# A Strassen FFN: stored block outputs added to x1 in DRAM, and the raw-weight rings at the change from plain tiles to blocks

## The chip, the cores and the metric

The kernel runs on 1 core of one Trainium2 chip. The metric is the device time of one execution in microseconds. Three runs of the kernel before took 898.76, 900.21 and 903.96 us; the median is 900.21.

## The reference

The layer is a hybrid of pooling mixer and mLSTM, followed by a SwiGLU FFN. All of the change is in the FFN's half, so the rest is named and left out:

```python
D_MODEL, SEQ = 1024, 512
D_FF = -(-8 * D_MODEL // (3 * 256)) * 256      # 2816 = 22 tiles of 128

def _swiglu(h, w_in, w_out):
    g, u = jnp.split(h @ w_in, 2, axis=-1)
    return (jax.nn.silu(g) * u) @ w_out
...
x1 = x + gate1 * (mixer(...) @ w_out_proj)
h  = _modulate(_rmsnorm(x1, ...), shift2, scale2)
x  = x1 + gate2 * _swiglu(h, w_ffn_in, w_ffn_out)
out = final rmsnorm(x)
```

## The kernel before

Every fp32 product is made from two rounded parts, high and low: three matmuls, wh·ah, wh·al and wl·ah (`mm3`). ScalarE casts the high part, VectorE subtracts it to get the low one (L158/L159, L177/L178, `split`); for some parts ScalarE writes the negated high part and an accumulating DMA of GpSimd's queue (POOL) adds the raw weight from DRAM (L1035/L1036, `direct` with a name in `sent`).

The FFN's 22 tiles of d_ff go in these steps. Tiles 0 to 2 are made with plain matmuls. Every later pair (one d_ff tile, gate and up rows together) is a `Pair`: seven products in the manner of Strassen instead of eight, four in `front` (A11, S1, S2, A12) and three in `back` (S3, S4, A22), of 12 matmuls of 128x256 each. `prepare` loads its two raw weights (`wr`, a ring of 3, and `ur`, a ring of 2) and makes seven high/low parts. Tile 3 is the pair `third`. Then a plain product brings tiles 0 to 3 through w_ffn_out into x1: for each of its 8 row blocks j a chunk of 512 columns is loaded into `wr` (into `ur` for j = 0), and the updated x1[j] is stored to DRAM as x1d[j] (L1443/L1446). Behind it x1's buffers close and those of the blocks open.

Two blocks follow, of the d_ff tiles from c0 = 4 and c0 = 10 on: three times an `Even` and an `Odd` pair (called E4, O5, and so on here), whose results are seven operand sets in `bo`, and then four `Out` pairs, which are the Strassen product with w_ffn_out over these six tiles. Their rows are scaled and stored to DRAM as od[c0] (L1236, L1240). The low part of A11 comes by accumulating DMA too for an `Odd` behind the block's first (L1179). Then come six plain pairs, P16 to P21, and a last plain product with the weights wl_0 to wl_7 over their tiles, with the final norm. For that, x1 is loaded back from x1d (L1472, two row blocks after each of P17 to P20), and 16 accumulating DMAs add od[4] and od[10] into it in SBUF (L1477), all issued behind P21's A22.

What sets the order: each engine runs its instructions in program order. `run` writes out the pairs so that a pair's front goes between the back products of the pair ahead, and prepares one pair ahead. Outside the part under `manual_schedule` a scheduler places the instructions on the engines; `issue_after` holds a group back until a named instruction. SP issues the plain loads and POOL the accumulating ones and the stores, each in its own order, and an instruction that waits there (for a buffer to come free) holds all behind it.

Names and lines: L188 to L190 are the matmuls of `mm3`; L1049 and L1050 VectorE's sums for S1 and S2 from `ur` and `wr`, L1056/L1057 those for S3/S4; L1124 VectorE's sum after S3, L1129 the one after S4, L1133 the one after A22, which ends a plain pair's value before its split into `act`; L1415 the update of x1.

## Time and profile before

| what | value |
|---|---|
| median of 3 runs | 900.21 us (898.76 to 903.96) |
| the profiled execution's own time | 899.67 us |
| its span | 897.9 us |
| PE busy | 874.6 us |
| mean granted clock of PE | 0.993 |
| DMA traffic | 134.59 MB, mean 150 GB/s |

The profile's times are of one execution and count from the span's start. A row of a timeline has start, duration, engine, line, operation, output<-input, and in brackets the idle time of the engine just before it with what ended it. PE is TensorE's matmuls, PEld its weight loads, DVE is VectorE, ACT ScalarE, POOL GpSimd. SPq is the queue of DMA issues on SyncE; its times are issues, not landings. A row of DMA issues has the transfer, the count, the size and the microseconds from issue to landing.

In the profile the plain product runs from about 573 to 603 us, the first block to about 690, the second to about 780, the pairs P16 to P21 to about 850.

### The profile page before, as it was taken

Reading aid. Unit: us, or ns where it says so; the run is one execution under the profiler, and the core shown is the slowest. Engines: PE = TensorE matmul, PEld = TensorE weight load, DVE = VectorE, ACT = ScalarE, POOL = GpSimd, SP = SyncE. Lnnn points to the kernel's source line nnn. Section 1 sums busy time; section 2 is a strip of 40 time slices with the busy share of each in tenths; the row PEclk is TensorE's granted clock in tenths of the full one; section 3 lists DMA queues with packets and bytes.
Section 4 is the critical chain, followed back from the end, with each engine's and each line's share of the span. In section 5 each row is a group of like instructions: output and inputs, shape, how many; then the busy total and the mean of one; then the engine's idle time right before and its main releaser. Section 6 shows DMA issues by size and latency. Waiting matters only on the chain.

```text
span 897.9 us, 15849 instructions
## 1 busy us (share of the span) xinstructions
PE 874.6 (97%) x6112; PEld 805.4 (90%) x6112; DVE 652.8 (73%) x1292; ACT 470.7 (52%) x919; POOL 98.1 (11%) x137
## 2 busy tenths in 40 slices
PE   9999999999999999999999999999999999998896
PEld 8689798899889998889988899879999999998896
DVE  4678677768876788667886659578888788856544
ACT  4454453545445453354545456446757775755442
POOL 0000000110000100001000000031202220221510
PEclk9999999999999999999999999999999999998999
DMA  9863021445352642526354710379637863794862
GB/s 350 317 201 99 25 71 60 164 129 153 106 177 66 194 112 76 191 69 199 98 153 154 276 48 25 94 211 239 142 103 218 218 147 99 223 283 103 181 127 95
DMA packets 48557, 134.59 MB, mean 150 GB/s; under 512 B 5440, under 2 KB 9824, under 8 KB 47456
## 3 DMA queue, kind: packets, MB, share of 16 engines
q1 hardware_dynamic: 38208, 112.06, 39.0%
q0 software_dynamic: 10272, 21.50, 11.7%
q8 instruction: 48, 0.79, 0.3%
q14 instruction: 29, 0.24, 0.1%
HBM read 123.56 MB, written 9.98 MB: 149 GB/s over the span
## 4 chain that ended last, share of the span: by engine, by line
PE 85%; DVE 6%; DMA 3%; ACT 3%; issue 2%; DVEq 0%; SPq 0%; ACTq 0%
PE ps L188 10%; PE ps L189 10%; PE ps L190 10%; PE ps L198 8%; PE ps L195 8%; PE ps L196 8%; PE pat L348 3%; PE ps L579 3%; PE ps L580 3%; PE ps L581 3%; PE pat L189 2%; PE pat L188 2%; PE pat L190 2%; PE pat L793 2%; PE pat L795 2%
## 5 line engine op out<-in xcount | busy, mean ns | idle before, releaser
L195 PE MATMUL ps<-a,wh 128*128 128x512 f32 x272 | 106.5, 392 | 0.0
L196 PE MATMUL ps<-a,wh 128*128 128x512 f32 x272 | 106.3, 391 | 0.0
L158 ACT CAST wh<-wr 128x1024 fp32r<-128x1024 f32 (+3 forms) x69 | 66.7, 969 | 63.4 <-PE ps L196 34.8
L159 DVE TENSOR_TENSOR wl<-wr,wh 128x1024 fp32r<-128x1024 f32 (+3 forms) x69 | 78.2, 1133 | 28.7 <-ACT wh L158 17.5
L198 PE MATMUL ps<-a,wl 128*128 128x512 f32 x272 | 68.0, 391 | 0.0
L196 PEld LDWEIGHTS ps<-a,wh 128*128 128x128 f32 x272 | 51.1, 188 | 10.2
L198 PEld LDWEIGHTS ps<-a,wl 128*128 128x128 f32 x272 | 50.9, 188 | 10.4
L195 PEld LDWEIGHTS ps<-a,wh 128*128 128x128 f32 x272 | 51.1, 188 | 10.1
L188 PE MATMUL ps<-hp,oh 128*128 128x256 f32 x176 | 50.8, 289 | 8.7 <-DVE tmp L1124 8.1
L1036 POOL DMA_DIRECT2D ol<-in_wffi x42 | 37.1, 882 | 146.6 <-ACT ol L1035 61.5
L188 PE MATMUL ps<-hp,gh 128*128 128x256 f32 x176 | 49.8, 283 | 2.9 <-ACT pat L1086 2.9
L190 PE MATMUL ps<-hp,ol 128*128 128x256 f32 x176 | 50.3, 286 | 0.0
L189 PE MATMUL ps<-hp,oh 128*128 128x256 f32 x176 | 50.2, 285 | 0.0
L189 PE MATMUL ps<-hp,gh 128*128 128x256 f32 x176 | 49.0, 278 | 0.0
L190 PE MATMUL ps<-hp,gl 128*128 128x256 f32 x176 | 48.9, 278 | 0.0
L177 ACT CAST gh<-sg 128x1024 fp32r<-128x1024 f32 (+1 forms) x27 | 26.7, 989 | 41.5 <-DVE sg L1050 26.5
L538 DVE SCALAR_TENSOR_TENSOR pb<-pb,crow_s 128x1024 f32<-128x1024 f32 x32 | 39.1, 1239 | 11.9 <-DMA pb<-in_wada_b 11.8
L188 PEld LDWEIGHTS ps<-hp,oh 128*128 128x128 f32 x176 | 34.6, 197 | 9.4 <-DVE tmp L1124 8.5
L793 PE MATMUL pat<-vh,Sp 128*128 128x258 f32 x144 | 41.1, 285 | 0.0
L794 PE MATMUL pat<-vl,Sp 128*128 128x258 f32 x144 | 40.7, 283 | 0.0
L795 PE MATMUL pat<-vh,Sp 128*128 128x258 f32 x144 | 40.7, 282 | 0.0
L178 DVE TENSOR_TENSOR gl<-sg,gh 128x1024 fp32r<-128x1024 f32 (+1 forms) x27 | 30.9, 1145 | 11.6 <-ACT gh L177 11.6
(422 smaller groups left out, 3031.2 us busy)
## 6 DMA issues: line engine op xcount, KB each, us to landing
wr<-in_w SPq DMA_DIRECT2D x42, 512.0 KB, 3.6
pb<-in_wada_b SPq DMA_DIRECT2D x32, 512.0 KB, 4.3
wr<-in_wffi SPq DMA_DIRECT2D x25, 512.0 KB, 4.8
ol<-in_wffi POOLq DMA_DIRECT2D x42, 256.0 KB, 5.8
ur<-in_wffi SPq DMA_DIRECT2D x19, 512.0 KB, 4.2
ada<-in_wada_a SPq DMA_DIRECT2D x8, 1024.0 KB, 9.9
wr<-in_wffo SPq DMA_DIRECT2D x16, 384.0 KB, 5.2
wr<-in_wout SPq DMA_DIRECT2D x8, 512.0 KB, 3.7
```

The source lines that it names most:

```text
L158: nc.scalar.copy(wh, raw[:, :n])
L159: V.tensor_sub(wl, raw[:, :n], wh.bitcast(F32))
L188: nc.tensor.matmul(dst, wh, ah, start=first and i == 0, stop=False, skip_group_check=on)
L189: nc.tensor.matmul(dst, wh, al, start=False, stop=False, skip_group_check=on)
L190: nc.tensor.matmul(dst, wl, ah, start=False, stop=last and i == n - 1, skip_group_check=on)
L195: nc.tensor.matmul(dst, wh, ah, start=first and i == 0, stop=False)
L196: nc.tensor.matmul(dst, wh, al, start=False, stop=False)
L198: nc.tensor.matmul(dst, wl, ah, start=False, stop=last and i == len(wparts) - 1)
L538: V.scalar_tensor_tensor(wa[:, :D], wa[:, :D], 0.5, crow_s, ALU.mult, ALU.mult, accum_out=mods[:, i:i + 1])
L793: nc.tensor.matmul(o, sh_, vh[:, s, :], start=n == 0, stop=False)
L794: nc.tensor.matmul(o, sh_, vl[:, s, :], start=False, stop=False)
L795: nc.tensor.matmul(o, sl_, vh[:, s, :], start=False, stop=n == len(srcs) - 1)
```

## The change

Four things change.

1. The stored rows od[c] are no longer added to x1 in SBUF. They are added to x1d in DRAM, by accumulating DMAs of POOL's queue, two row blocks at a time: od[4] behind the A22 part of the second block's E12, O13, E14 and O15, od[10] behind that of P18 to P21.
2. x1 is loaded from x1d once, complete, by eight loads that are held back behind the first load of P21.
3. The plain product's raw chunks for j = 3 to 7 go to `tmp` buffers instead of `wr`; the first pair of the first block is prepared inside that loop (at j = 6), and the items are made ahead of it. The matmuls of j = 2 are held back behind the last matmul of `third`.
4. In `run`, at the change from pairs to `Out`, the three back products of the last odd pair go one by one around the first front products of the first `Out`, not after two of them. In `prepare`, `ur` is loaded ahead of `wr`.

```diff
@@ prepare
-        nc.sync.dma_start(b, wb)
-        p["loaded"] = nc.sync.dma_start(a, wa)
+        p["loaded"] = nc.sync.dma_start(b, wb)
+        nc.sync.dma_start(a, wa)
@@ Pair.back
-            mm3(x, p["A22"], b["T4"], first=False, on=True)
+            self.end = mm3(x, p["A22"], b["T4"], first=False, on=True)
@@ run
             joint = isinstance(it, Out) and not isinstance(prev, Out)
+            if joint:
+                next(b)
             if not it.begun:
                 next(f)
+                if joint:
+                    next(b)
                 next(f)
             if joint:
-                for _ in b:
-                    pass
+                next(b)
@@ the plain product of tiles 0 to 3
-        mm3_low_last(acc, wf[j][:NP], act[:NP], last=False)
+        with tc.issue_after(third.end.ins) if j == 2 else ExitStack():
+            mm3_low_last(acc, wf[j][:NP], act[:NP], last=False)
...
     for j in range(3, KT):
-        ffn_out(j, ALL, wchunk(j, 0, c1), 0, c1)
+        if j == 6:
+            made(items[0])
+        ffn_out(j, ALL, wchunk(j, 0, c1, raw=S("tmp")), 0, c1)
         nc.gpsimd.dma_start(x1d[j], x1[j])
...
-    back_ = iter(range(KT))
+    rows = {c: iter(range(KT)) for c in od}
@@ also
-        elif it in plain:
-            with tc.issue_after(plain[min(plain.index(it) + 1, len(plain) - 1)].p["loaded"].ins):
-                for j in itertools.islice(back_, 2):
+        middle = items[11:15]
+        if it in middle or it in plain[1:5]:
+            c = 4 if it in items else 10
+            now = (items + plain)[(items + plain).index(it) + 1]
+            with tc.issue_after(now.p["added"].ins):
+                for j in itertools.islice(rows[c], 2):
+                    nc.gpsimd.dma_start(x1d[j], od[c][j], accum_op=ALU.add, max_dma_last_dim=2048)
+        if it is plain[-2]:
+            with tc.issue_after(plain[-1].p["loaded"].ins):
+                for j in range(KT):
                     nc.sync.dma_start(x1[j], x1d[j])
-        if it is plain[-2]:
-            with tc.issue_after(plain[-1].p["added"].ins):
-                for j in range(KT):
-                    for c in (4, 10):
-                        nc.gpsimd.dma_start(x1[j], od[c][j], accum_op=ALU.add)
-
-    made(items[0])
```

**SP's queue near the end.** Of the kernel before, from the fifth x1 load on (`wr_9532` is P21's, `ur_9401` P20's, `ur_9533` P21's; the two `in_wffo` loads are wl_0 and wl_1; four x1 loads stand right ahead of these rows):

```order
L1472 DMA x_1495_9132<-x1d 128x512
L1472 DMA x_1496_9133<-x1d 128x512
L1019 DMA wr_9532<-in_wffi 128x1024
L1472 DMA x_1497_9134<-x1d 128x512
L1472 DMA x_1498_9135<-x1d 128x512
L1018 DMA ur_9401<-in_wffi 128x1024
L155 DMA wr_9829<-in_wffo 128x768
L1018 DMA ur_9533<-in_wffi 128x1024
L155 DMA wr_9835<-in_wffo 128x768
```

Of the changed kernel, the same queue from P20's `ur_9409` on (`ur_9541` is P21's):

```order
L1019 DMA ur_9409<-in_wffi 128x1024
L155 DMA wr_9829<-in_wffo 128x768
L1019 DMA ur_9541<-in_wffi 128x1024
L1487 DMA x_1491_9136<-x1d 128x512
L1487 DMA x_1492_9137<-x1d 128x512
L155 DMA wr_9835<-in_wffo 128x768
```

The x1 loads have moved from ahead of P20's `ur` to behind P21's. They continue in pairs among the final weights; this is how they stand around wl_3 (`wr_9847`) and wl_4 (`wr_9853`) now:

```order
L1487 DMA x_1495_9140<-x1d 128x512
L1487 DMA x_1496_9141<-x1d 128x512
L155 DMA wr_9847<-in_wffo 128x768
L1487 DMA x_1497_9142<-x1d 128x512
L1487 DMA x_1498_9143<-x1d 128x512
L155 DMA wr_9853<-in_wffo 128x768
```

Each of these x1 loads waits in the queue for the addition of od[10] to its row block in x1d.

**POOL's queue in the second block.** Before, from E12's A22 on (`ol_7929`), through O13's A11, A12 and A22 to E14's A12 (`ol_8182`):

```order
L1036 DMA ol_7929<-in_wffi 128x512
L1036 DMA ol_8036<-in_wffi 128x512
L1036 DMA ol_8047<-in_wffi 128x512
L1036 DMA ol_8059<-in_wffi 128x512
L1036 DMA ol_8182<-in_wffi 128x512
```

In the changed kernel at the same place:

```order
L1037 DMA ol_7929<-in_wffi 128x512
L1483 DMA x1d<-od_5502 128x512 x2
L1037 DMA ol_8038<-in_wffi 128x512
L1037 DMA ol_8049<-in_wffi 128x512
L1037 DMA ol_8061<-in_wffi 128x512
L1483 DMA x1d<-od_5502 128x512 x2
L1037 DMA ol_8186<-in_wffi 128x512
```

Pairs of additions (`od_5502` is od[4]) now stand between the A22 of one pair and the first low part of the next, which is A11 for O13; two more pairs follow in the same way, the first of them ahead of O15's A11.

**VectorE at the change point.** Before, around the end of `third` (`tmp_6308` and `tmp_6346` are its values, `act_6349` its low part; `sg_6561<-ur_6558` is E4's first sum; `wl_6425` and `wl_6455` are the plain product's chunks 2 and 3):

```order
L1124 TENSOR_TENSOR tmp_6308<-ps_6274,tmp_6308 128x256
L1049 TENSOR_TENSOR sg_6561<-ur_6558 128x512
L159 TENSOR_TENSOR wl_6395<-wr_6392,wh_6394 128x512
L1129 SCALAR_TENSOR_TENSOR tmp_6346<-tmp_6308,tmp_6346 128x256
L1133 SCALAR_TENSOR_TENSOR tmp_6346<-ps_6274,tmp_6346 128x256
L178 TENSOR_TENSOR act_6349<-tmp_6346,act_6348 128x512
L1415 SCALAR_TENSOR_TENSOR x_925_5300<-ps_6275,lb,x_925_5300 128x512
L159 TENSOR_TENSOR wl_6425<-wr_6422,wh_6424 128x512
```

In the changed kernel (`ur_6513` and `wr_6512` are E4's raw weights, `ur_6590` and `wr_6589` those of O5):

```order
L1130 SCALAR_TENSOR_TENSOR tmp_6346<-tmp_6308,tmp_6346 128x256
L1051 TENSOR_TENSOR sg_6516<-sg_6516,wr_6512 128x512
L1058 TENSOR_TENSOR sg_6532<-sg_6516,wr_6512 128x512
L178 TENSOR_TENSOR gl_6524<-sg_6516,gh_6523 128x1024
L1050 TENSOR_TENSOR sg_6593<-ur_6590 128x512
L1134 SCALAR_TENSOR_TENSOR tmp_6346<-ps_6274,tmp_6346 128x256
L1051 TENSOR_TENSOR sg_6593<-sg_6593,wr_6589 128x512
L178 TENSOR_TENSOR act_6349<-tmp_6346,act_6348 128x512
L1034 TENSOR_TENSOR ol_6595<-wr_6589,oh_6594 128x512
```

E4's sums and two sums of O5 now stand ahead of the last steps of `third` (L1134 and the split into `act_6349`), and so ahead of the updates of x1.

## Prediction

> **What bounds the kernel now.** I read the page's busy times first, then what PE (TensorE) waited for after 566 us, since the order of the two programs is the same before that.

> ```profile
> PE 874.6 (97%) x6112; PEld 805.4 (90%) x6112; DVE 652.8 (73%) x1292; ACT 470.7 (52%) x919; POOL 98.1 (11%) x137
> PE ps L188 <- DVE tmp L1124: 8.1, 2, 4.8
> PE ps L188 <- ACT pat L1086: 2.9, 4, 1.6
> PE ps L188 <- ACT bo L177: 1.2, 2, 0.6
> PE ps L188 <- ACT act L177: 1.2, 1, 1.2
> PE ps L188 <- DVE x L1415: 0.6, 1, 0.6
> ```

> PE is busy 97% of the span, and the change takes no matmul away and adds none. So only PE's idle time and clock can move: the waits rows (total, times, longest) add up to 14.0 us, and 8.1 of them are two waits for one line. The timeline of PE says where they stand; the bracket is the idle time before the instruction.

> ```profile
> 582.66 0.73 PE L188 MATMUL ps<-act,wh 128*128 128x512 f32 x2 [1.17 <-ACT act L177]
> 608.31 0.39 PE L188 MATMUL ps<-hp,gh 128*128 128x256 f32 x1 [1.63 <-ACT pat L1086]
> 723.80 0.39 PE L188 MATMUL ps<-hp,gh 128*128 128x256 f32 x1 [0.47 <-ACT pat L1086]
> 812.08 0.58 PE L188 MATMUL ps<-hp,oh 128*128 128x256 f32 x1 [4.82 <-DVE tmp L1124]
> 850.59 0.58 PE L188 MATMUL ps<-hp,oh 128*128 128x256 f32 x1 [3.27 <-DVE tmp L1124]
> ```

> The change meets four places: the wait at 812, the one at 850, the odd pairs of the second block (700 to 745), and the change point from plain product to blocks (570 to 610). I take them in the order of their size.

> **The wait at 812: x1 loaded late.** Timelines of SP's queue and VectorE, the transfer issued at 799 and the page's median of all such, and windows (length, busy PE, PEld, DVE, ACT, POOL, clock, DMA share, GB/s):

> ```profile
> 790.84 3.84 SPq L1472 DMA_DIRECT2D x<-x1d  x6
> 799.35 0.33 SPq L1018 DMA_DIRECT2D ur<-in_wffi  x1
> ur<-in_wffi SPq DMA_DIRECT2D x1, 512.0 KB, 10.8
> ur<-in_wffi SPq DMA_DIRECT2D x19, 512.0 KB, 4.2
> 810.27 0.69 DVE L1049 TENSOR_TENSOR sg<-ur 128x512 f32<-128x512 f32 x1 [7.75 <-DMA ur<-in_wffi]
> 812.08:814.00 1.92, 1.92 (x9) 1.92 (x10) 1.43 (x3) 1.92 (x4) 0.00 (x0) 0.50 0.00 0
> 814.00:818.00 4.00, 4.00 (x27) 4.00 (x27) 4.00 (x8) 3.35 (x8) 0.88 (x1) 0.71 0.45 101
> ```

> The x1 loads (six in this row, two just after) go out ahead of P20's `ur`, which then takes 10.8 us and lands at 810.15. VectorE stands 7.75 us before its sum, and behind that sum in its order is L1124, for which PE waits. Without the wait PE goes on 4.82 us earlier, so `ur` has 10.8 - 4.8 = 6.0 us to land. In the new order all x1 loads stand behind P21's `ur`, the last Strassen load, and nothing but P21's `wr` and P20's low parts is near. The median of such loads is 4.2 us, and two DRAM additions beside it at 800.5 and 801.4 (behind P18's A22) can cost it 1.6 us at most at the price below: 5.8, in time. The wait goes, and the slow clock behind it: 1.92 x 0.50 + 4.00 x 0.29 = 2.1 us. Together **-6.9**. Kept for the range: 0 to -6.9.

> **The wait at 850: the fifth final weight.**

> ```profile
> 835.75 0.87 POOL L1036 DMA_DIRECT2D ol<-in_wffi  x1 [6.78 <-ACT tmp L1121]
> 836.29 3.93 POOL L1477 DMA_DIRECT2D x<-od  x4
> 842.21 1.69 SPq L155 DMA_DIRECT2D wr<-in_wffo  x2
> wr<-in_wffo SPq DMA_DIRECT2D x1, 384.0 KB, 6.0
> wr<-in_wffo SPq DMA_DIRECT2D x1, 384.0 KB, 3.2
> ol<-in_wffi POOLq DMA_DIRECT2D x1, 256.0 KB, 4.1
> 848.26 0.62 ACT L171 CAST oh<-wr 128x512 fp32r<-128x512 f32 x1 [4.68 <-DMA wr<-in_wffo]
> 850.50:854.00 3.50, 3.41 (x16) 3.41 (x17) 2.96 (x7) 1.49 (x4) 1.05 (x2) 0.52 1.13 203
> ```

> wl_4 is issued at 842.21 and, under the 16 additions of od into x1, lands 6.0 us later at 848.2 (the 3.2 is the same size issued at 834.20, into quiet). ScalarE's cast then holds what PE needs, so PE resumes 2.4 us after the landing; it would go on at 847.32. The change takes these 16 additions away, but puts x1[6] and x1[7] ahead of wl_4 on SP. Both wait for the last two DRAM additions, which POOL issues behind P21's A22 low part: at 836.65 and 837.55. That low part lands at 839.9 (4.1 us), and at 1.6 us each (worked out in the next part) the additions land near 841.5 and 843.1. SP then issues the last x1 load and wl_4, at about 843.8 with 0.35 us each; with 3.2 us alone and 1.6 for the 512 KB ahead of it in the same queue, it lands near 848.6, and a wait within 0.6 of the old one follows. A wait for a busy queue becomes one for a late issue: at most **+0.6**, which I take, and the slow clock (3.41 x 0.48 = 1.6 us) stays. Bounds: additions that land by 842.3 give 846 and a wait of 1.1, no slow clock: -3.8; additions of 3.2 us each, +3.8.

> **The second block's odd pairs: DRAM additions in POOL's queue.** POOL and PE timelines, transfers, queue and window over 700 to 745:

> ```profile
> 710.17 0.89 POOL L1036 DMA_DIRECT2D ol<-in_wffi  x1 [5.81 <-ACT tmp L1121]
> 711.48 0.87 POOL L1036 DMA_DIRECT2D ol<-in_wffi  x1 [0.42 <-DVE ev L1133]
> ol<-in_wffi POOLq DMA_DIRECT2D x1, 256.0 KB, 6.7
> 719.25 0.28 PE L190 MATMUL ps<-hp,ol 128*128 128x256 f32 x1
> 730.91 0.87 POOL L1036 DMA_DIRECT2D ol<-in_wffi  x1 [0.45 <-DVE ev L1133]
> ol<-in_wffi POOLq DMA_DIRECT2D x1, 256.0 KB, 6.0
> 739.21 0.28 PE L190 MATMUL ps<-hp,ol 128*128 128x256 f32 x1
> q0 software_dynamic: 1760, 3.43, 41.2%
> 700.00:745.00 45.00, 44.53 (x389) 44.32 (x388) 36.84 (x64) 31.53 (x60) 10.77 (x13) 1.00 0.76 173
> ```

> Between 710.17 (A22 of E12) and 711.48 (A11 of O13) POOL now issues two additions, and two more between the same places of E14 and O15. The pairs behind O13 and O15, and the four of c=10, stand ahead of low parts that are needed much later. An addition is 0.88 us of issue and p us of its queue. p isn't in the trace (no transfer here goes from DRAM to DRAM). From 13 transfers at 41.2% of 45 us: 18.5 / 13 = 1.43 us of all engines, if nothing else is on them. Lower bound 0.8 us (256 KB at the 324 GB/s of a window below), upper 3.2 (both sides in DRAM, twice an addition with one). I take **1.6**, a little over the 1.43, since plain loads run beside it. A11's low part of O13 landed at 718.2, 1.05 us before its first use at 719.25: it becomes 2p - 1.05 late, of which the 0.47 at 723.80 is swallowed. That of O15 landed at 736.9, 2.3 us before use: 2p - 2.3. Together 4p - 3.8 = **+2.6** (0 at 0.95 or less, +9.0 at 3.2, with slow clocks 3 us more). The window's DMA share goes from 0.76 by 8 x 1.43 / 45 = 0.25 to about 1.0, which speaks for lateness.

> [...]

> **The change point.** Timelines and windows:

> ```profile
> 572.16 1.81 SPq L1018 DMA_DIRECT2D ur<-in_wffi  x2
> 581.53 0.42 DVE L1133 SCALAR_TENSOR_TENSOR tmp<-ps,tmp 128x256 f32<-128x256 f32 x1 [3.69 <-PE ps L190]
> 582.64 0.69 DVE L178 TENSOR_TENSOR act<-tmp,act 128x512 fp32r<-128x512 f32 x1 [0.68 <-ACT act L177]
> 574.00:578.00 4.00, 4.00 (x29) 3.67 (x28) 2.14 (x4) 0.91 (x2) 0.00 (x0) 1.00 0.89 253
> 608.00:610.00 2.00, 1.69 (x14) 1.69 (x15) 2.00 (x3) 1.35 (x4) 0.00 (x0) 1.00 1.07 324
> ```

> With the chunks for j = 3 to 7 in `tmp`, `wr` and `ur` of the first two pairs are loaded ahead of and among these chunks in SP's order, not behind them. What it gains: the waits of 0.6 (L1415, at 603) and 1.63 (608), where the first pairs' parts came late: **-2.3**, as E4 and O5 are then prepared while the plain product still runs. What it costs: in VectorE's order the sums of O5 (from `ur`, then from `wr`) now stand ahead of L1134 and of `act`'s low part, which end at 581.95 and 583.33 in these rows and waited for PE and ScalarE alone. Ahead of O5's `wr` and with it are 0.26 MB of a low part, three times 0.52 and five times 0.26 (`tmp`): 3.15 MB from about 574 on (the quiet 384 KB above took 3.2 us, 1.2 of them at 324 GB/s, so some 2 us from issue to flow). At 253/0.89 = 284 GB/s they land at 585.1, at 324 at 583.7; I take the middle, 584.4. Two VectorE instructions of 0.69 follow, so the low part is there at 585.8, 2.4 us late: **+2.4**. PE's wait is then 1.17 + 2.4 = 3.6 in two pieces; 3.27 had a slow clock after it and 1.63 had none (1.00 in the row of 608), so half of 1.6: **+0.8**. Sum of the place **+0.9**; -2.3 if the loads land by 582, +5 at 250 GB/s with the slow clock.

> [...]

> **Back products ahead of Out's A11.** The waits for `bo` (1.2 in all) end with a low part that VectorE makes after the same matmuls as before; I put it at 0, 0.6 either way each. The swapped issue of `ur` and `wr` costs nothing: both sums that read them need both.

> **Sum:** -6.9 + 0.6 + 2.6 + 0.9 + 0 = -2.8. The profiled execution took 899.67 (span 897.9 and 1.8 around it), 0.5 below the median of 900.21: 896.9 against it, **897.4** as a median.

> **Rivals.**
> 1. *Everything lands in time*: additions at 1 us or less, the change point's loads by 582. Then -6.9 - 2.3 - 3.5 (at 850) = -12.7: 887.5. For it: 4.2 us is the median of loads of 512 KB, so most run undisturbed. Against it: 1.43 us for an addition with one side in DRAM, and the DMA share of 1.0.
> 2. *Slower: the price of a DRAM addition.* Place: POOL's queue, ahead of A11 of O13 and O15, and ahead of x1[6], x1[7], wl_4. The sum goes as 6p - 12.4 (four times p at the odd pairs, twice at 850), is zero at 2.1 us, and with a slow clock of 1.6 after O13's wait passes +4.5 at 2.6. At p = 2.8 it is 4.4 and, with a slow clock after O15's wait too, 4.4 + 1.6 + 1.6 = +7.6: 907.8. [...]
> 3. *The wait at 812 stays by half* because the additions of 800.5 and 801.4 fall on P20's `ur`, as x1 did: -3 in place of -6.9, so 901. For it: 10.8 us when 2 MB were ahead; against it: only 0.5 MB now.

> **How the numbers follow.** Forecast 0.45 (own range 892 to 902), rival 1 0.25, rival 2 0.16, rival 3 0.14. 0.5% (4.5 us) is about what a measurement of this kernel can tell from no change. Faster than 895.7: all of rival 1 and a third of the forecast, 0.40. Slower than 904.7: nearly all of rival 2 and little else, 0.17. Within: 0.43. The range reaches from 886 to 908, below rival 1 and to the price of 2.8 us.

> **What the changed profile would show.** No wait at L1125 near 812, and full clock there; `ur` of P20 landing within 6 us. A wait at L1125 near 850 whose releaser's load is issued at 843 to 845. Two waits for `ol` before PE's L191 of A11 at about 719 and 740, of 2 and 1 us. At 582 a wait of some 3 us behind VectorE's sum of O5, and none at 603 and 608. What would make it wrong: landings of DRAM additions much nearer or further apart than 1.6 us, or loads at the change point that end before 582.

## The result, and the profile after

| | before | after |
|---|---|---|
| median of 13 runs | 899.09 us | 905.21 us |
| lowest run | 895.5 | 902.08 |
| span of the profiled execution | 897.9 | 903.5 |
| PE's granted clock, mean | 0.993 | 0.988 |

The ratio of after to before is 1.0068 with a 95% interval of 1.0044 to 1.0091: slower by 0.7%, where the forecast had 0.3% faster. The time lies within the range of 886 to 908, but on the other side of the kernel before. One of the 13 runs before, of 1075.31 us, was a slow one, and the ratio leaves it out.

The same views of the changed kernel: the page's busy times, the waits of PE after 560 us (total, times, longest), and PE's timeline at the waits of over 1 us.

```profile
PE 877.8 (97%) x6112; PEld 808.6 (90%) x6112; DVE 653.7 (72%) x1292; ACT 472.4 (52%) x919; POOL 98.7 (11%) x137
PE ps L188 <- ACT act L177: 6.0, 1, 6.0
PE ps L188 <- ACT pat L1087: 4.4, 6, 3.1
PE ps L190 <- DMA ol<-in_wffi: 4.0, 2, 2.2
PE ps L188 <- DVE tmp L1125: 1.8, 1, 1.8
586.65 1.22 PE L188 MATMUL ps<-act,wh 128*128 128x512 f32 x2 [5.96 <-ACT act L177]
724.40 0.46 PE L190 MATMUL ps<-hp,ol 128*128 128x256 f32 x1 [2.18 <-DMA ol<-in_wffi]
747.36 0.38 PE L190 MATMUL ps<-hp,ol 128*128 128x256 f32 x1 [1.83 <-DMA ol<-in_wffi]
844.99 0.58 PE L188 MATMUL ps<-hp,gh 128*128 128x256 f32 x1 [3.10 <-ACT pat L1087]
858.12 0.39 PE L188 MATMUL ps<-hp,oh 128*128 128x256 f32 x1 [1.85 <-DVE tmp L1125]
```

The wait at 812 is gone, and so are those at 603 and 608. The one at 582 has grown from 1.17 to 5.96 us, and that for final weight 4 (at 850 before, now at 858) has shrunk from 3.27 to 1.85. Three are new: 724 and 747 in the odd pairs, and 845. To see what each place is worth, one matches the same instruction of both kernels. POOL's DMA issues serve (start in us):

```
                                     before    after   after - before
last low part ahead of the change    567.43   566.81    -0.6
low part at the first block's end    642.75   645.80    +3.0
E12's A22                            710.17   713.15    +3.0
E14's A22                            729.59   735.74    +6.2
low part behind the second block     792.89   802.49    +9.6
P19's A22                            815.38   819.76    +4.4
P20's A22                            825.36   828.47    +3.1
the last instruction of the norm     889.59   895.60    +6.0
```

So the change point costs 3.6, the odd pairs 6.6, the place at 812 gains 6.5 in two steps, and the final weights cost 2.9. The forecast had +0.9, +2.6, -6.9 and +0.6 for these four. Three readings of the new waits follow. First the change point, VectorE's timeline and windows (length, busy PE, PEld, DVE, ACT, POOL, clock, DMA share, GB/s):

```profile
584.91 0.69 DVE L1050 TENSOR_TENSOR sg<-ur 128x512 f32<-128x512 f32 x1 [4.09 <-DMA ur<-in_wffi]
585.52 0.42 DVE L1134 SCALAR_TENSOR_TENSOR tmp<-ps,tmp 128x256 f32<-128x256 f32 x1
586.31 0.69 DVE L1051 TENSOR_TENSOR sg<-sg,wr 128x512 f32<-128x512 f32 x1 [0.36 <-DMA wr<-in_wffi]
586.92 0.68 DVE L178 TENSOR_TENSOR act<-tmp,act 128x512 fp32r<-128x512 f32 x1
586.00:588.00 2.00, 1.35 (x3) 0.85 (x4) 1.69 (x3) 2.00 (x4) 0.00 (x0) 0.50 0.92 375
588.00:592.00 4.00, 4.00 (x11) 3.09 (x11) 3.19 (x6) 2.30 (x4) 1.77 (x3) 0.57 0.17 71
```

VectorE stands 4.09 us for O5's `ur`, and only behind that sum comes L1134, the step of the third pair that ScalarE's cast and then PE need. The wait is 4.8 us longer than before, and the slow clock behind it loses 1.35 x 0.50 + 4.00 x 0.43 = 2.4 us more. With the 2.3 of the waits at 603 and 608 taken off, these make 4.9, where the matched rows have 3.6; a wait of 0.66 at 634 went as well, and the rest isn't traced.

The odd pairs: POOL's timeline, transfers from issue to landing (E12's A22, O13's A11, O15's A11), windows behind the two waits.

```profile
713.15 0.89 POOL L1037 DMA_DIRECT2D ol<-in_wffi  x1 [5.91 <-ACT tmp L1122]
713.73 2.04 POOL L1483 DMA_DIRECT2D x1d<-od  x2
714.81 2.79 POOL L1037 DMA_DIRECT2D ol<-in_wffi  x2
ol<-in_wffi POOLq DMA_DIRECT2D x1, 256.0 KB, 6.0
ol<-in_wffi POOLq DMA_DIRECT2D x1, 256.0 KB, 9.5
ol<-in_wffi POOLq DMA_DIRECT2D x1, 256.0 KB, 9.9
724.30:728.00 3.70, 3.60 (x17) 3.60 (x18) 1.67 (x4) 1.57 (x3) 0.34 (x1) 0.54 1.08 271
747.30:751.00 3.70, 3.64 (x21) 3.64 (x22) 2.42 (x5) 1.73 (x3) 0.63 (x1) 0.66 1.08 220
```

E12's A22 lands at 719.15, O13's A11 at 724.3 with two DRAM additions between them: 5.2 us for three transfers, 1.7 each. Behind both waits the clock was low: 3.60 x 0.46 = 1.7 us and 3.64 x 0.34 = 1.2.

The final weights: SP's queue, the load of weight 2, the additions issued just ahead of it (median of two), ScalarE's cast of it, and the two windows behind PE's wait.

```profile
828.74 2.19 SPq L1487 DMA_DIRECT2D x<-x1d  x2
831.31 0.47 SPq L155 DMA_DIRECT2D wr<-in_wffo  x1
wr<-in_wffo SPq DMA_DIRECT2D x1, 384.0 KB, 8.9
x1d<-od POOLq DMA_DIRECT2D x2, 256.0 KB, 9.3
840.30 0.84 ACT L177 CAST gh<-wr 128x768 fp32r<-128x768 f32 x1 [8.44 <-DMA wr<-in_wffo]
844.99:847.00 2.01, 2.01 (x9) 2.01 (x10) 0.73 (x2) 0.24 (x1) 1.28 (x2) 0.50 0.81 121
847.00:851.00 4.00, 4.00 (x21) 4.00 (x20) 1.39 (x2) 1.53 (x2) 0.00 (x0) 0.52 0.82 134
```

Final weight 2 takes 8.9 us. ScalarE waits 8.44 for it with its cast, and everything that PE needs from ScalarE for P21 stands behind: the wait of 3.10 at 844.99 and a half clock behind it.

### The profile page after: what moved, and what is told of

The parts are those of the page before. It is cut to its first block, busy times and chain, and to the rows that moved or that the text cites. A ratio compares the mean times of both kernels' runs of the same rounds, so it can differ in the third digit from the quotient of the medians.

```text
span 903.5 us, 15838 instructions
## 1 busy us (share of the span) xinstructions
PE 877.8 (97%) x6112; PEld 808.6 (90%) x6112; DVE 653.7 (72%) x1292; ACT 472.4 (52%) x919; POOL 98.7 (11%) x137
## 3 DMA queue, kind: packets, MB, share of 16 engines
HBM read 123.56 MB, written 14.17 MB: 152 GB/s over the span
## 4 chain that ended last, share of the span: by engine, by line
PE 83%; DMA 5%; ACT 4%; DVE 4%; issue 2%; POOL 0%; SPq 0%; DVEq 0%; ACTq 0%
PE ps L188 11%; PE ps L190 10%; PE ps L189 10%; PE ps L199 8%; PE ps L197 8%; PE ps L196 8%; PE pat L349 3%; PE ps L580 3%; PE ps L581 3%; PE ps L582 3%; DMA ol<-in_wffi 2%; PE pat L189 2%; PE pat L188 2%; PE pat L190 2%; PE pat L794 2%
## 5 line engine op out<-in xcount | busy, mean ns | idle before, releaser
L159 DVE TENSOR_TENSOR wl<-wr,wh 128x1024 fp32r<-128x1024 f32 (+3 forms) x64 | 74.6, 1165 | 30.1 <-ACT wh L158 18.8
L158 ACT CAST wh<-wr 128x1024 fp32r<-128x1024 f32 (+3 forms) x64 | 63.7, 995 | 53.9 <-PE ps L197 34.8
L188 PE MATMUL ps<-hp,gh 128*128 128x256 f32 x176 | 51.5, 293 | 4.4 <-ACT pat L1087 4.4
L1037 POOL DMA_DIRECT2D ol<-in_wffi x42 | 39.8, 978 | 136.2 <-ACT ol L1036 66.8
L190 PE MATMUL ps<-hp,ol 128*128 128x256 f32 x176 | 49.7, 282 | 4.0 <-DMA ol<-in_wffi 4.0
L188 PE MATMUL ps<-hp,oh 128*128 128x256 f32 x176 | 49.6, 282 | 1.8 <-DVE tmp L1125 1.8
L189 PE MATMUL ps<-hp,gh 128*128 128x256 f32 x176 | 50.3, 286 | 0.0
L190 PE MATMUL ps<-hp,gl 128*128 128x256 f32 x176 | 50.3, 286 | 0.0
L189 PE MATMUL ps<-hp,oh 128*128 128x256 f32 x176 | 49.3, 280 | 0.0
L177 ACT CAST gh<-sg 128x1024 fp32r<-128x1024 f32 (+1 forms) x27 | 26.7, 988 | 35.9 <-DVE sg L1051 20.5
L188 PE MATMUL ps<-act,wh 128*128 128x256 f32 (+1 forms) x109 | 35.6, 328 | 6.0 <-ACT act L177 6.0
L188 PEld LDWEIGHTS ps<-hp,gh 128*128 128x128 f32 x176 | 34.6, 197 | 5.9 <-ACT pat L1087 5.8
## 6 DMA issues: line engine op xcount, KB each, us to landing
wr<-in_w SPq DMA_DIRECT2D x42, 512.0 KB, 3.6
pb<-in_wada_b SPq DMA_DIRECT2D x32, 512.0 KB, 4.4
wr<-in_wffi SPq DMA_DIRECT2D x25, 512.0 KB, 4.5
ol<-in_wffi POOLq DMA_DIRECT2D x42, 256.0 KB, 6.4
ur<-in_wffi SPq DMA_DIRECT2D x19, 512.0 KB, 4.1
wr<-in_wffo SPq DMA_DIRECT2D x16, 384.0 KB, 4.3
wr<-in_wout SPq DMA_DIRECT2D x8, 512.0 KB, 3.6
```

Source lines behind the costliest of these rows:

```text
L158: nc.scalar.copy(wh, raw[:, :n])
L159: V.tensor_sub(wl, raw[:, :n], wh.bitcast(F32))
L188: nc.tensor.matmul(dst, wh, ah, start=first and i == 0, stop=False, skip_group_check=on)
L189: nc.tensor.matmul(dst, wh, al, start=False, stop=False, skip_group_check=on)
L190: end = nc.tensor.matmul(dst, wl, ah, start=False, stop=last and i == n - 1, skip_group_check=on)
L1037: p["added"] = nc.gpsimd.dma_start(tiled(l), dram, accum_op=ALU.add)
```

## The experiments

Every ratio is to the kernel before, with its 95% interval; the changed kernel has 1.0068 [1.0044, 1.0091] and a span of 903.5. The last four rows rest on 4 runs each, the others on 9 or 10. A span is that of one profiled execution, and it need not lie near the middle of its runs.

| run | ratio | span |
|---|---|---|
| O5's preparation held | 0.9999 [0.9978, 1.0021] | 900.1 |
| change point as before | 1.0006 [0.9988, 1.0024] | 903.3 |
| all od[4] additions behind O15 | 1.0059 [1.0039, 1.0079] | 904.4 |
| od[4] additions behind A11 | 1.0026 [1.0013, 1.0040] | 900.9 |
| x1 loads on POOL's queue | 1.0044 [1.0023, 1.0066] | 899.7 |
| no od[10] additions | 0.9972 [0.9955, 0.9989] | 897.3 |
| od[10] added in SBUF | 1.0039 [1.0026, 1.0052] | 901.9 |
| final weights 4 to 7 prepared late | 0.9998 [0.9978, 1.0018] | 900.9 |
| all repairs joined | 0.9856 [0.9840, 0.9872] | 886.1 |
| joined, change point as before | 0.9849 [0.9828, 0.9869] | 886.6 |
| kernel before, x1 late | 0.9917 [0.9895, 0.9939] | 891.4 |
| kernel before, x1 late, weights late | 0.9856 [0.9837, 0.9875] | 885.4 |

### The change point: O5's preparation held

```diff
+            chunk[:] = nc.scalar.copy(wh, raw[:, :n]), V.tensor_sub(wl, raw[:, :n], wh.bitcast(F32))
...
             if after:
-                made(after)
+                with ExitStack() as st:
+                    for i in hold if it is items[0] else ():   # chunk 3's cast and subtraction
+                        st.enter_context(tc.issue_after(i.ins))
+                    made(after)
```

> The changed kernel, with O5's preparation on VectorE and ScalarE held behind the cast and subtraction of the plain product's fourth chunk; its loads stay where they are. Theory (order on VectorE): PE's wait of 5.96 us at 587 comes from O5's sums, whose raw weights land at 584.8 and 586.3, standing ahead of the last steps of the third pair. Then the wait is about 1.2 again, the slow clock behind it (about 2.4 us) goes, and the span is some 7 us shorter than 903.5, 896 to 897. Rival (volume): the loads themselves, five chunks and three pairs' raw weights, hold up whatever PE needs next; then a wait of 4 us or more stays in 580 to 592 with another releaser and the span stays above 901.

PE's timeline of this run:

```profile
578.60 0.50 PE L197 MATMUL ps<-act,wh 128*128 128x512 f32 x1 [1.37 <-ACT wh L158]
583.63 0.73 PE L189 MATMUL ps<-act,wh 128*128 128x512 f32 x2 [1.27 <-ACT act L178]
```

The loads are the same, and the wait is 1.27 instead of 5.96, with a new one of 1.37 ahead of it. The order on VectorE made it, not the volume. The ratio fell by 0.7%, close to the 7 us that were expected; the span, 900.1, missed the 896 to 897, because in this execution the wait for weight 4 was 2.94 us with a clock of 0.68 in the 4 us behind it, not 1.85 with 1.00.

### The change point as before

```diff
-        if j == 6:
-            made(items[0])
-        ffn_out(j, ALL, wchunk(j, 0, c1, raw=S("tmp")), 0, c1)
+        ffn_out(j, ALL, wchunk(j, 0, c1), 0, c1)
...
+    made(items[0])
     for _ in run(items + plain, also=also).back():
```

> The changed kernel with the plain product as before it: chunks 3 to 7 in wr, the first pair prepared behind the loop, no holding back of the third chunk's matmuls. Theory (order on VectorE): PE waits 1.2 us at 582 with no slow clock, and the two waits near 603 and 608 (0.6 and 1.6) are back: 903.5 - 4.8 - 2.4 + 2.3, span 898 to 899, about 1 to 2 us behind the run that only holds O5's preparation. Rival (the early loads are worth nothing): the same time as that run within 0.5 us.

```profile
581.70 0.73 PE L188 MATMUL ps<-act,wh 128*128 128x512 f32 x2 [1.17 <-ACT act L177]
602.64 0.39 PE L188 MATMUL ps<-hp,oh 128*128 128x256 f32 x1 [0.64 <-DVE x L1419]
607.62 0.38 PE L188 MATMUL ps<-hp,gh 128*128 128x256 f32 x1 [1.62 <-ACT pat L1087]
```

All three waits are as expected, so loading early does remove 0.6 and 1.6. The profiled execution missed its 898 to 899 by over 4 us, again by waits elsewhere (2.47, 2.24, 3.21 and 3.56 us at the odd pairs and the final weights, with clocks of 0.59, 0.66, 0.62 and 0.60 in the 4 us behind them). In time the two ways can't be told apart (1.0006 and 0.9999 with intervals of 0.2% either way), which is what the rival said; the pair of joined versions below asks again.

### The od[4] additions moved in POOL's queue, twice

```diff
# all behind O15
-        middle = items[11:15]
-        if it in middle or it in plain[1:5]:
+        if it is items[14] or it in plain[1:5]:
...
-                for j in itertools.islice(rows[c], 2):
+                for j in itertools.islice(rows[c], 8 if c == 4 else 2):
```

> The changed kernel, with all eight additions of od[4] into x1d issued in a row behind O15's last low part instead of in pairs behind E12, O13, E14 and O15. Theory (order in POOL's queue): the two waits of PE for ol at 724 and 747 (2.18 and 1.83 us) and the slow clock behind each (about 1.7 and 1.3) go: 6 to 7 us, span 896.5 to 897.5. Rival (DMA time): the 256 KB additions take their time from other transfers wherever they stand; then waits for weights of the Out pairs of 2 us or more appear between 748 and 775, and the span gains less than 3.

```diff
# behind A11 (p["sent0"] is a pair's first accumulating DMA)
-        if it in middle or it in plain[1:5]:
+        if it in items[12:15] or it in plain[1:5]:
...
-            with tc.issue_after(now.p["added"].ins):
+            for key in ("sent0", "added") if it is items[14] else ("sent0",) if c == 4 else ("added",):
+                with tc.issue_after(now.p[key].ins):
```

> The changed kernel, with the od[4] additions issued one or two places later in POOL's queue: behind the A11 low part of O13 and O15, behind E14's A12, and the last pair behind O15's A22. Same transfers in the same stretch. Theory (order in POOL's queue): O13's and O15's A11 low parts land about 3.2 and 4.2 us earlier, the two waits for ol and the slow clock behind them go and nothing takes their place: 6 us, span 897 to 898. Rival (DMA time, as the run with all eight behind O15 suggests, where waits of 2.1 and 0.7 us came up among the Out pairs): other transfers of 712 to 748 become late and the span stays above 901.

The run with all eight behind O15: PE's largest wait between 740 and 790, and VectorE's ahead of it:

```profile
758.70 0.56 DVE L1050 TENSOR_TENSOR sg<-ur 128x384 f32<-128x384 f32 x1 [3.92 <-DMA ur<-in_wffo]
763.24 0.38 PE L188 MATMUL ps<-bo,gh 128*128 128x256 f32 x1 [2.10 <-ACT bo L177]
```

In both runs the two waits for `ol` are gone. With eight additions in a row a wait of 2.10 came back among the Out pairs: VectorE stood 3.92 us for a raw weight of theirs that was issued behind the additions (0.20 in the changed kernel). The ratio hardly moved (1.0059). One place later in the queue, behind the one low part that was urgent, nothing came back: the largest wait of PE between 700 and 800 is 0.62, and the ratio falls by 0.4% to 1.0026. That is less than the 6 us expected, and the span of 900.9 lies above the 897 to 898: behind this place the wait for weight 4 was 3.22 us, and the clock 0.57 in the 4 us after it, in this execution. The order in the queue is the cause of the two waits; DMA time is the cost of piling the additions up.

### Final weight 2: x1's loads or the additions

```diff
# x1 loads on POOL's queue, behind the last addition
-            with tc.issue_after(plain[-1].p["loaded"].ins):
+            with tc.issue_after(last[0].ins):
                 for j in range(KT):
-                    nc.sync.dma_start(x1[j], x1d[j])
+                    nc.gpsimd.dma_start(x1[j], x1d[j])
```

> The changed kernel, with the eight loads of x1 moved from SP's queue, where they stand in pairs among the final weights, to POOL's, behind the last addition of od[10]. Theory (x1 loads in SP's order): the new wait of 3.10 us at 845 (final weight 2 lands 8.9 us after its issue) and its slow clock of about 2.9, and the wait of 1.85 at 858 go: 6 to 8 us, span 896 to 897.5. Rival (the additions): the DRAM additions and low parts of POOL's queue at 828 to 832 make final weight 2 late; then it still takes 7 us or more, a wait of 2 us or more stays at 845, and only the wait at 858 goes: span 901 or more.

```diff
# no od[10] additions
-                for j in itertools.islice(rows[c], 2):
+                for j in itertools.islice(rows[c], 2 if c == 4 else 0):
```

> The changed kernel without the additions of od[10] into x1d (the second block's contribution is left out of the output); the x1 loads stay in SP's queue and wait for nothing there but the additions of od[4]. Theory (x1 loads in SP's order, by what they wait for): final weight 2 is still issued at the same place, but the x1 loads ahead of it have gone 6 to 8 us earlier, it lands within 5 us, and the waits at 845 and 858 go: 896 to 897.5. Rival (bytes of x1 ahead of the weight): it still takes 7 us and the wait at 845 stays with 2 us or more. With the run that moves the x1 loads to the other queue: gone in both is the pair of them together, gone in this one alone is the additions, gone in the other alone is the bytes.

```diff
# od[10] in SBUF, as before
-        if it in middle or it in plain[1:5]:
+        if it in middle:
...
+            with tc.issue_after(plain[-1].p["added"].ins):
+                for j in range(KT):
+                    nc.gpsimd.dma_start(x1[j], od[10][j], accum_op=ALU.add)
```

> The changed kernel, with od[10] added to x1 in SBUF behind P21's last low part, as before the change; od[4] is still added in DRAM and x1 loaded once behind P21's first load. Theory: final weight 2 is late because the od[10] additions are in the queues at 820 to 832 and hold x1's loads ahead of it, so without them there it lands within 5 us and the wait of 3.10 at 845 with its slow clock (6.0 together) goes. The additions now lie over final weight 4, so its wait is between the 1.85 of the change and the 5.2 of the run with x1 on POOL's queue, say 3.3 with a slow clock of 1.6: net 3 us shorter, span 900 to 901. Rival (x1's bytes): eight loads of x1 now stand in a row ahead of final weight 1, so a wait of 2 us or more for it or weight 2 appears between 825 and 845 and the span is above 903.

ScalarE's cast of final weight 2 in the three runs, in this order, and PE's waits behind it in the first:

```profile
833.87 0.84 ACT L177 CAST gh<-wr 128x768 fp32r<-128x768 f32 x1 [7.01 <-DMA wr<-in_wffo]
838.56 0.39 PE L188 MATMUL ps<-hp,gh 128*128 128x256 f32 x1 [1.08 <-ACT pat L1087]
852.25 0.58 PE L188 MATMUL ps<-hp,oh 128*128 128x256 f32 x1 [5.16 <-DVE tmp L1125]
```

```profile
836.82 0.84 ACT L177 CAST gh<-wr 128x768 fp32r<-128x768 f32 x1 [5.44 <-DMA wr<-in_wffo]
850.69 0.38 PE L188 MATMUL ps<-hp,oh 128*128 128x256 f32 x1 [0.42 <-DVE tmp L1125]
```

```profile
836.87 0.83 ACT L177 CAST gh<-wr 128x768 fp32r<-128x768 f32 x1 [5.40 <-DMA wr<-in_wffo]
854.77 0.38 PE L188 MATMUL ps<-hp,oh 128*128 128x256 f32 x1 [4.41 <-DVE tmp L1125]
```

ScalarE's idle time of 8.44 falls to 7.01 without x1's loads ahead, and to 5.4 without the DRAM additions, where the eight x1 loads go out earlier in one row; at 5.4 PE no longer waits near 845. The five other runs that leave this place as it is have 7.47 to 9.16 here, and waits of PE of 2.41 to 3.23, so 7.01 alone would say little, but 1.08 and 5.4 lie clear of them. So neither theory has it alone: the additions weigh more. How much of that they do as transfers in the queues, and how much by making x1's loads wait until they stand right ahead of the weight, the runs don't separate. The gain of moving the loads was 0.2%, since the wait for weight 4 grew to 5.16 under what now lies over it. The same happens with od[10] in SBUF (4.41): my forecast of 3.3 for it was too low, and the ratio is 1.0039.

### Final weights 4 to 7 prepared behind P21's last split

```diff
-    wl_ = [wchunk(j, c0, c1, (...)[j]) for j in range(KT)]
+    wl_, behind = [], tuple(made_)      # cast and subtraction of the last split
+    for j in range(KT):
+        with ExitStack() as st:
+            for i in behind if j >= 4 else ():
+                st.enter_context(tc.issue_after(i.ins))
+            wl_.append(wchunk(j, c0, c1, (...)[j]))
```

> The changed kernel, with the preparation of final weights 4 to 7 on ScalarE and VectorE held behind the last split of P21; their loads stay. Theory: the wait of 1.85 us at 858 (and 3.27 in the kernel before) is only the place of final weight 4 in VectorE's order, ahead of the sum that PE waits for; it goes entirely, and with it 1.9 us: span about 901.6. Rival: that weight is needed soon itself, so the wait moves to the final product (a wait of over 1 us for a weight after 865) and the span stays within 0.5 of 903.5. The wait at 845 stays in both.

No wait remains between 846 and 870, and none came for a weight in the final product. The ratio falls by 0.7%, far more than 1.9 us. The profiled execution of the changed kernel was a mild one at this place: four runs whose code is the same there (O5 held, change point as before, and both with the od[4] additions moved) waited 2.94, 3.56, 3.82 and 3.22 us, with clocks of 0.68, 0.60, 0.58 and 0.57 in the 4 us behind. That makes some 5 us likely for most executions, though waits aren't known of executions without a profile.

### All together, and the kernel before with two repairs

> All repairs together: O5's preparation held at the change point, od[4] additions behind the A11 low parts, od[10] added in SBUF, final weights 4 to 7 prepared behind the last split. Theory (four separate causes, each a place in a queue): the gains add up: 7 at the change point's wait and clock, of which the first run of this edit got 5.6 in the time, 6 at the odd pairs, 6 at 845, 1.9 at 858: 903.5 less 19.5 to 21, span 883 to 885 and ratio to the kernel before 0.983 to 0.987. Rival (one cause, DMA time between 570 and 860): what is won in one place comes back in the next, the span is 890 or more and the ratio above 0.991.

> The joined version with the plain product as before the change (chunks in wr, first pair prepared behind the loop). What the reworked change point is worth once O5's sums don't stand in the way. Theory: the waits near 603 and 608 are back, 2.3 us: span 888 to 889 against 886.1. Rival: loading ahead is worth nothing, the same time within 0.5 us.

```diff
# kernel before, x1 late: ur ahead of wr in prepare as in the change, and
-        elif it in plain:
-            with tc.issue_after(plain[min(plain.index(it) + 1, len(plain) - 1)].p["loaded"].ins):
-                for j in itertools.islice(back_, 2):
-                    nc.sync.dma_start(x1[j], x1d[j])
         if it is plain[-2]:
+            with tc.issue_after(plain[-1].p["loaded"].ins):
+                for j in range(KT):
+                    nc.sync.dma_start(x1[j], x1d[j])
```

> The kernel before the change with one part of it alone: ur ahead of wr in prepare, and x1 loaded complete behind P21's ur; all 16 additions of od into x1 in SBUF as before. Theory: the wait of 4.82 at 812 and its slow clock (2.1) go, the wait for final weight 4 near 845 stays at 3 to 5 us with its slow clock: 897.9 less 6 to 7, span 891 to 892, ratio 0.992 to 0.993. Rival: 2 MB of x1 now stand ahead of final weights 1 and 2, PE waits 2 us or more for them between 825 and 845, and the span is 895 or more.

> As the run with x1 late in the kernel before, and the preparation of final weights 4 to 7 held behind P21's last split. Theory: the second wait goes with its clock too, 4.9 us more: span 886 to 887, ratio 0.986 to 0.988, no DRAM addition needed. Rival (DMA): with 16 additions in SBUF over 836 to 862 final weights 4 to 7 or x1 itself come late for the final product and a wait of over 1 us appears behind 855: span 889 or more.

All waits of PE after 560 us in the joined version:

```profile
PE ps L190 <- ACT pat L1090: 3.9, 8, 0.9
PE ps L190 <- ACT act L180: 1.2, 1, 1.2
PE ps L191 <- DVE bo L180: 0.6, 2, 0.3
PE pat L192 <- DMA ol<-in_wffi: 0.2, 1, 0.2
```

PE waits 5.9 us in all and the clock is 0.999: the gains add up, at 0.9856 as expected (the span is 1 us above the expected range), so they are separate places in queues and not one shared lack of DMA time. With the old change point the joined version is as fast (0.9849, a span of 886.6 where 888 to 889 was expected), so its rival came true: in time, loading ahead is worth nothing that 4 runs could tell. Its waits of 1.55 and 0.23 near 605 are matched by smaller ones of the reworked version elsewhere. And the kernel before with only x1's loads late (and `ur` ahead of `wr`) has 0.9917; with the final weights held too it has 0.9856. Those two edits are worth as much as the whole joined version, without a single addition in DRAM.

## Why the prediction was wrong

**Which step failed.** The step on final weight 4: "The change takes these 16 additions away, but puts x1[6] and x1[7] ahead of wl_4 on SP." The same order puts x1[2] and x1[3] ahead of weight 2, and other additions of od[10] into the queues at that time; the prediction weighed only the weight that was late before, and its sum has no term for weight 2. Weight 2 is cast on ScalarE ahead of P21's front, so its lateness reached PE: 3.10 of wait and, at 0.50 and 0.52 of the clock, 2.01 x 0.50 + 4.00 x 0.48 = 2.9 more, against nothing in the sum. The two experiments without the od[10] additions at this time show it: no such wait remains.

**Two terms were mis-sized**, and by size they are the larger part: of the 9.4 us between the forecast's -2.8 and the +6.6 of the matched rows, 4.0 are the odd pairs, 2.7 the change point, 2.3 the final weights and 0.4 the place at 812. The odd pairs were put at 2.6 and cost 6.6. The price of a DRAM addition was right at O13 (1.6 taken; with the shift of the queue taken off, its A11 landed 3.1 us later than in the kernel before, for two additions), and so was the first wait (2.15 in the sum, 2.18 measured). At O15 the same landing came 4.2 us later, 2.1 for each addition, and the second wait was 1.83 instead of 0.9. What was left out is the low clock, 1.7 and 1.2 us, which the sum put behind neither wait. The change point was put at +0.9 and cost 3.6: the loads landed later than the 584.4 of the sum (O5's `ur` by 584.9 and its `wr` by 586.3, where the slower of the two rates gave 585.1), so the wait grew by 4.8 and not 2.4, and the clock lost all of 2.4 and not 0.8. The mechanism there, O5's sums ahead of the last steps of the third pair, is shown by the run that holds them.

**What was right.** The wait at 812 went with its clock, 6.5 against 6.9 forecast, and x1 late in the kernel before, with `ur` ahead of `wr`, gives that without the other parts (0.9917). The waits near 603 and 608 went. The wait for weight 4 stayed, 1.85 to 3.8 us against the 3.9 that its +0.6 stood for. Back products ahead of Out's A11 were worth little, as forecast: waits of 0.59 and 0.58 near 661 and 751 became one of 0.31.

**The rivals.** The second had the side and the places right but not the mechanism: the price of an addition is well short of its 2.6 us. The doubling behind the bound of 3.2 (both sides in DRAM) was the author's estimate and no run shows it: behind two additions the landings came 3.1 and 4.2 us later, and the pages of both kernels have 123.56 MB read from HBM, with 14.17 MB written after the change and 9.98 before. The time came from the sum of smaller things that the forecast had each at its friendly end, in particular the clock: 2.9 us at the odd pairs, 2.9 behind the wait for weight 2 and 1.6 more than taken at the change point.

## What to carry to other kernels

A load that is moved in a queue is weighed against every load that it is moved past, and each of those against what stands behind its first use on the engine that casts it; the one that was late before isn't the only one that can be late. An early load brings its first use forward in the scheduler's order too, and a use that comes too early holds back work that was ready; holding that use to its old place kept the gain. A queue's order can be mended by one place, behind the one urgent transfer; moving everything to a quiet stretch filled that stretch. And a new wait of some 2 us is priced with the slow clock that may follow it, which here cost nearly as much again (1.7 us behind a wait of 2.18).

## What was not expected of the hardware

```profile
745.05:748.46 3.41, 1.57 (x14) 1.38 (x13) 2.98 (x8) 1.52 (x4) 2.58 (x3) 1.00 1.08 247
748.46:751.87 3.41, 3.41 (x18) 3.41 (x18) 2.17 (x3) 2.05 (x4) 0.00 (x0) 0.50 1.10 193
854.27:857.68 3.41, 2.00 (x18) 1.80 (x16) 1.25 (x3) 1.90 (x5) 0.00 (x0) 1.00 0.58 220
857.68:861.10 3.42, 2.98 (x26) 2.99 (x27) 3.19 (x8) 1.59 (x5) 0.00 (x0) 1.00 0.43 131
720.32:723.74 3.42, 1.60 (x15) 1.40 (x13) 3.42 (x7) 2.62 (x5) 1.99 (x3) 1.00 1.10 236
723.74:727.15 3.41, 2.95 (x25) 2.95 (x26) 1.63 (x4) 1.72 (x4) 0.58 (x1) 1.00 1.09 281
```

The wait of 1.83 falls whole into one step, PE is idle for 1.84 of 3.41 us, and the next step is slow (0.50). The waits of 1.85 and 2.28 are cut in two by the steps, at most 1.41 and 1.82 of one step are idle, and the next one has 1.00. Of the steps at full clock in the traces of the two kernels (from 30 us on), all eight with 1.84 us or more of idle PE were followed by a slow one, and none with less was, of which the largest has 1.63. So in these executions a wait of nearly the same length cost 1.7 us of clock (3.41 x 0.50) or nothing by where it lay among the steps: 1.83 at the second odd pair did, and the changed kernel's 1.85 for weight 4 did not. Why the clock has such steps, no run shows.
